# A streaming encoder layer whose five queues are ordered by a pass over the traced instructions, by the longest way to the end

## The chip, the core and the metric

The kernel runs on one core of one Trainium2 chip. A core has five engines with a queue of their own, each worked off in order: TensorE (PE in the profile, with PEld for its weight loads), VectorE (DVE), ScalarE (ACT), GpSimd (POOL) and SyncE (SP), which here issues every DMA. The engines wait for each other through semaphores. The metric is the device time of one execution in microseconds (us), lower being better.

## What is computed

One step of a one-layer hybrid encoder, in float32, for 1024 new tokens of one stream and 32 tokens of a running one, 1056 rows of 1024 numbers:

```python
h = rms_norm(x) @ w_in                      # 15 pieces: q, k, v and gates of three kinds of heads
o_a = gated_linear_scan(q, k, v, log_a)     # GLA, 6 heads:    S_t = diag(a_t) S_{t-1} + k_t v_t^T, o_t = S_t^T q_t
o_b = gated_linear_scan(q, k, v, log_f)     # HGRN2, 5 heads:  the same, wider keys
o_c = mlstm_scan(q, k, v, log_f, ig)        # mLSTM, 5 heads, stabilised by a running maximum
cat = [head_norm(o_a)*silu, head_norm(o_b)*silu, head_norm(o_c)*sigmoid]
x = x + rms_norm(cat @ w_out)
up = causal_conv(rms_norm(x) @ w_up)        # 1024 -> 2 x 2816, width 3
x = x + rms_norm((gelu(gate) * val) @ w_down)
```

The two outputs are returned with all the final states of the recurrences and the convolutions.

## The kernel before

Every big product is made of three matmuls on numbers split into a high and a low half (`mm3`, lines 100 to 102: high by high, high by low, low by high); `split` makes the halves on ACT (L106) and DVE or POOL (L108, L109).

The work runs in stages. `inproj` projects the normed tokens in three groups of 384, 384 and 256+32 tokens: `norm_group` transposes them (tiles xt), `feat` makes 13 feature tiles (PSUM tiles pf, written pf1_6 for group 1, tile 6), and `vg` or `vg_across` eight blocks of values and gates (pv, for group 2 also the transposes pb). Each group's results go to DRAM. `mixer(u, g, ci0)` reads them back for one unit of 128 tokens (u is 0 to 7, and 8 for the 32 tokens of the other stream) and does the scans. Its long part are six levels of scores within a chunk (widths 32, 16, 8, 4, 2, 1; PSUM tiles sc0_32 to sc0_1 for unit 0): for each, DVE and ACT make decayed copies of queries and keys (x, Ld, Qz), PE makes 16 narrow matmuls of 64 rows, and DVE puts them into the score matrix P under a mask (L782). Then come the outputs (og, oh), the mLSTM part (sm, mi, oi, om) and the normed result, cat. The narrow matmuls are issued through `first` and all carry line 692. The tiles that a unit reads (qkb, mqk, v, gt) have one buffer each, the scores one PSUM buffer, and the state goes from one unit to the next, so the units follow each other.

`outproj(p2, W, u)` transposes a unit's cat (ctp), multiplies it with w_out (zp, two halves of 512 columns), norms it, adds x, norms again and transposes for the FFN (fxt). `up_all` makes the up projection by 22 pairs of column tiles and two token halves, each as seven block products (PSUM tiles puy, pux, puw, puz), a convolution on ACT and DVE (y) and the gelu product, stored to h_d. `down_all` reads h_d back and sums over 22 tiles in PSUM (pd).

The order of the work came from two places. The program is written by generators that are pulled in turn: `merge(main, nmain, nside)` advances a list of pending mixers beside the projections, so that group 1 is projected while group 0 is mixed, group 2 while group 1 is mixed, and the output projection runs beside the last units. The scheduler of the tile layer (with `schedule_with_timeline_sim=True`) then lists the instructions of each engine by a simulation of its own, and takes hints from the code: `tc.high_priority(offset=...)` around the narrow matmuls and one logarithm, and `tc.issue_after(ins)`, which keeps a block behind another instruction.

```python
    def first(fn, *args, **kw):
        with tc.high_priority(offset=AHEAD):
            fn(*args, **kw)
```

Of the kernel before, what the change touches and what calls it, by code (L numbers as in the profile page):

```python
# [1 line left out]

# [6 lines left out]
F32 = mybir.dt.float32  # L9
# [3 lines left out]
AF = mybir.ActivationFunctionType  # L13
ALU = mybir.AluOpType
PSUM = bass.MemoryType.PSUM
DRAM = bass.MemoryType.DRAM
# [74 lines left out]
def body(ctx: ExitStack, tc: tile.TileContext, a: dict):  # L91
    nc = tc.nc
    act, dve, pool, pe, sp = nc.scalar, nc.vector, nc.gpsimd, nc.tensor, nc.sync
# [76 lines left out]
    vecs = const("vecs_sb", [128, 12], F32, a["vecs"])  # L170
# [5 lines left out]
    caus, rmask, self_ = cf[:, 0:64], cf[:, 64:448], cf[:, 448:832]  # L176
# [36 lines left out]
    oml = const("oml", [128, 4])  # L213
# [127 lines left out]
    def out_units(g, dst, dst_s, rng, src, smp_off=None, rows=slice(0, 128), drows=None):  # L341

        t0, pl, sl = GROUPS[g]
        u0, nu = t0 // 128, pl // 128
        drows = rows if drows is None else drows
        sp.dma_start(dst[(slice(u0, u0 + nu), drows) + rng].rearrange("u p n -> p u n"),
                     src[rows, :pl].rearrange("p (u n) -> p u n", n=128))
        if sl:
            so = pl if smp_off is None else smp_off
            sp.dma_start(dst_s[(drows,) + rng], src[rows, so:so + sl])  # L350

    def inproj(g, xh, xl, normed, scaled=None):
        t0, pl, sl = GROUPS[g]
        T = pl + sl
# [132 lines left out]
        fr4, e8 = (pf.tile([128, m, T], F32, tag=t, name=f"{t}_{g}", bufs=1) for (t, m) in (("fr", 4), ("e", 8)))  # L487
        e4, fx4, er = e8[:, 0:4], e8[:, 4:7], e8[:, 7]
# [11 lines left out]
                dve.tensor_scalar(fx4[:, f - 1], fx4[:, f - 1], lb[:, f:f + 1], None, op0=ALU.mult)  # L500

        def logs():
            with tc.high_priority(offset=LNA):
                act.activation(e8, e8, AF.Ln, bias=1.0)

        def decays(f, ins):

            with tc.issue_after(ins.ins):
                fr, ls = fr4[:, f], e4[:, f]
                lo = (128, 0, 0, 64)[f]  # L510
                dve.scalar_tensor_tensor(ls, fr, 0.0, ls, op0=ALU.min, op1=ALU.subtract)
                if f:
                    dve.tensor_tensor(fr[lo:], ls[lo:], fr[lo:], op=ALU.subtract)
                    act.activation(fr[lo:], fr[lo:], AF.Exp)
                    dve.tensor_scalar(fr[lo:], fr[lo:], oml[lo:, f:f + 1], None, op0=ALU.mult)
                    dve.tensor_tensor(ls, ls, fx4[:, f - 1], op=ALU.add)
                    out_units(g, qkb_d, qkbs_d, (1, f, slice(None)), fr, None, slice(lo, 128))
                if f in (0, 3):
                    dve.tensor_scalar(ls, ls, vecs[:, 8 + f:9 + f], None, op0=ALU.mult)
                dve.tensor_tensor_scan(ls, rmask[:, :T], ls, 0.0, op0=ALU.mult, op1=ALU.add)  # L520
                out_units(g, qkb_d, qkbs_d, (2, f, slice(None)), ls)

        def store_q(f, q):
            out_units(g, qkb_d, qkbs_d, (0, f, slice(None)), q)
# [84 lines left out]
        for t, f in ((6, 1), (7, 2)):  # L609
            ps = feat(t)  # L610
# [14 lines left out]
        row = rows()  # L625
# [9 lines left out]
        q = t1("q", 2)  # L635
# [19 lines left out]
        for t, j in ((10, 0), (11, 1), (12, 2), (13, 3)):  # L655
            ins = conv(j, feat(t))
# [25 lines left out]
    halves, kwi = [], [None]  # L682
# [4 lines left out]
    AHEAD = 100  # L687
    LNA = 100

    def first(fn, *args, **kw):  # L690
        with tc.high_priority(offset=AHEAD):
            fn(*args, **kw)

    def mixer(u, g, ci0):
        n = 128 if u < 8 else DEC
        t0 = 128 * u
        chunks = [(0, 64), (64, 64)] if u < 8 else [(0, DEC)]
        cl = chunks[0][1]
# [49 lines left out]
        with ExitStack() as behind:  # L748
            if halves:

                for ins in (kwi[0], halves[1]):
                    behind.enter_context(tc.issue_after(ins.ins))
            spread(dve, qz, lambda r, fs, psl: dve.tensor_tensor(qz[r, psl, :n], q4[r, fs, :], eb4[r, fs, :],
                                                                 op=ALU.mult), n)
        kh = mx.tile([128, 512], F32, tag="x", name=f"kh{u}", bufs=NX)
# [3 lines left out]
                          b5, op=ALU.subtract)  # L759
# [31 lines left out]
        for c in levels:  # L791
            x = mx.tile([128, 512], F32, tag="x", name=f"x{u}_{c}", bufs=NX)
# [198 lines left out]

# [110 lines left out]
    def col_operands(pool_, q, s, between=lambda: None):  # L1102

        n = SUBS[s][1]
        res = {}

        def halves(name, src):
            p = pool_[name in ("T2", "T3")]
            h = p.tile([128, 4, n], F32R, name=f"{name}h{s}")
            l = p.tile([128, 4, n], F32R, name=f"{name}l{s}")  # L1110
            res[name] = h, l
            act.copy(h, src)
            return dve.tensor_tensor(l, src, h.bitcast(F32), op=ALU.subtract)
# [375 lines left out]
    p7s.close()  # L1489
    p4s.close()  # L1490

def _layout(i):
# [125 lines left out]
```

## Time and profile before

| what | us |
| --- | --- |
| timed runs, median (lowest to highest of 3) | 1444.28 (1443.7 to 1444.57) |
| profiled execution, span from first to last instruction | 1434.5 |
| PE busy | 1370.8 |
| DVE busy | 1008.9 |
| ACT busy | 713.2 |
| POOL busy | 274.1 |

The span is the time from the first to the last instruction of one profiled execution on the one core; what the timed runs have over it lies before and after. Busy time is the time in which at least one instruction of the engine is under way. The ends of matmuls are modelled, and a matmul's row holds the time until its result is there, so that rows of one engine overlap; the distance of two starts is then the cost of one. A line can be that of a helper: all big products have lines 100 to 102, all narrow ones 692.

### The profile page before, as it was taken

What the parts mean: (1) busy time and instruction counts of PE and PEld (TensorE: products, weight loads), DVE (VectorE), ACT (ScalarE), POOL (GpSimd) and SP (SyncE); (2) the same over time, 40 slices, a digit from 0 to 9 for tenths busy, and PEclk for the clock granted to TensorE, in tenths of its full rate; (3) what the DMA queues carried; (4) which work ended last, traced back from release to release, by engine and by line L of the source; (5) the groups of instructions that cost most, each with busy time, mean ns of one, the idle gap of its engine ahead of it and who ended that gap; (6) DMA issues with size and microseconds to landing.
All of it is one profiled execution on the core that took longest, in us unless ns stands there. A gap on an engine that the chain in (4) does not pass through costs nothing.

```text
span 1434.5 us, 30019 instructions
## 1 busy us (share of the span) xinstructions
PE 1370.8 (96%) x11804; PEld 1254.9 (87%) x11804; DVE 1008.9 (70%) x1826; ACT 713.2 (50%) x1403; POOL 274.1 (19%) x456
## 2 busy tenths in 40 slices
PE   7989999999998998999799999999999999999997
PEld 6989889898887986767699999999999999988785
DVE  5796478757596668676698888788878865654644
ACT  5545556445475545333665555455555545543432
POOL 6531121113021235212111111111111110000101
PEclk9999999999999999999899999999999999999999
DMA  9599778667789754344312221222122266665742
GB/s 344 190 317 351 263 251 300 221 228 241 236 279 329 250 181 148 109 147 111 122 49 98 79 90 61 90 75 82 68 90 75 75 211 227 222 214 170 247 168 103
DMA packets 132437, 255.11 MB, mean 178 GB/s; under 512 B 28647, under 2 KB 79367, under 8 KB 132295
## 3 DMA queue, kind: packets, MB, share of 16 engines
q1 hardware_dynamic: 132295, 253.19, 51.9%
q8 instruction: 92, 1.51, 0.4%
q14 instruction: 50, 0.41, 0.1%
HBM read 192.26 MB, written 60.89 MB: 176 GB/s over the span
## 4 chain that ended last, share of the span: by engine, by line
PE 73%; DVE 12%; ACT 5%; DMA 5%; issue 2%; POOL 1%; SPq 1%; DVEq 0%; ACTq 0%
PE pd L101 5%; PE pd L100 5%; PE pd L102 5%; PE pux L100 4%; PE pux L102 4%; PE pux L101 4%; PE pv L102 4%; PE pv L100 4%; PE pv L101 4%; PE puw L100 3%; PE puw L101 3%; PE puw L102 3%; DMA qkb<-qkb_d 2%; PE zp L100 2%; PE zp L101 2%
## 5 line engine op out<-in xcount | busy, mean ns | idle before, releaser
L1226 DVE SCALAR_TENSOR_TENSOR y<-uu,fconv_sb,y 128x1060 f32<-128x1060 f32 x88 | 116.2, 1321 | 27.4 <-ACT y L1224 26.6
L100 PE MATMUL pd<-wd,hh 128*128 128x512 f32 x264 | 104.5, 396 | 0.3 <-ACT hh L106 0.3
L101 PE MATMUL pd<-wd,hh 128*128 128x512 f32 x264 | 104.7, 397 | 0.0
L102 PE MATMUL pd<-wd,hl 128*128 128x512 f32 x264 | 90.5, 394 | 0.0
L1220 POOL COPY uu<-uu 128x2 f32<-128x2 f32 x44 | 30.5, 693 | 211.5 <-DVE uu L1188 211.4
L1183 ACT COPY c<-pux 128x274 f32<-128x274 f32 (+1 forms) x132 | 49.1, 375 | 41.4 <-PE pux L102 40.3
L1224 ACT ACTIVATE y<-uu,fconv_sb 128x1060 f32<-128x1060 f32 x44 | 56.1, 1275 | 18.6 <-POOL uu L1221 18.1
L100 PE MATMUL zp<-woh,ch 128*128 128x512 f32 (+1 forms) x144 | 58.3, 411 | 4.1 <-DVE cl L1020 3.1
L100 PEld LDWEIGHTS pd<-wd,hh 128*128 128x128 f32 x264 | 49.6, 188 | 13.1 <-ACT hh L106 0.9
L102 PEld LDWEIGHTS pd<-wd,hl 128*128 128x128 f32 x264 | 49.6, 188 | 11.9
L101 PEld LDWEIGHTS pd<-wd,hh 128*128 128x128 f32 x264 | 49.6, 188 | 11.5
L100 PE MATMUL pv<-wt_0h,xh 128*128 128x256 f32 (+2 forms) x195 | 57.1, 293 | 2.3 <-ACT xh L316 2.3
L101 PE MATMUL zp<-wol,ch 128*128 128x512 f32 (+1 forms) x144 | 58.6, 407 | 0.0
L102 PE MATMUL zp<-woh,cl 128*128 128x512 f32 (+1 forms) x144 | 58.0, 406 | 0.2 <-DVE cl L1020 0.2
L102 PE MATMUL pv<-wt_1h,xl 128*128 128x256 f32 (+2 forms) x195 | 56.9, 292 | 0.5 <-DVE xl L317 0.5
L102 PE MATMUL pv<-wt_0h,xl 128*128 128x256 f32 (+2 forms) x195 | 56.5, 290 | 0.6 <-DVE xl L317 0.6
L100 PE MATMUL pv<-wt_1h,xh 128*128 128x256 f32 (+2 forms) x195 | 56.7, 291 | 0.0
L101 PE MATMUL pv<-wt_1l,xh 128*128 128x256 f32 (+2 forms) x195 | 56.5, 290 | 0.0
L101 PE MATMUL pv<-wt_0l,xh 128*128 128x256 f32 (+2 forms) x195 | 56.2, 288 | 0.1
L101 PE MATMUL pd<-hl,wd 128*128 128x288 f32 x176 | 50.3, 297 | 0.6 <-DVE hl L109 0.6
L218 POOL TENSOR_SCALAR hrs<-hss 128x5 f32<-128x5 f32 (+3 forms) x27 | 13.9, 514 | 192.1 <-DVE hss L888 191.4
L102 PE MATMUL pd<-hh,wd 128*128 128x288 f32 x176 | 50.1, 296 | 0.0
(1668 smaller groups left out, 5162.7 us busy)
## 6 DMA issues: line engine op xcount, KB each, us to landing
h_d<-y SPq DMA_DIRECT2D x22, 530.0 KB, 2.9
wt_0r<-in_w_tok SPq DMA_DIRECT2D x21, 512.0 KB, 8.2
wt_1r<-in_w_tok SPq DMA_DIRECT2D x21, 512.0 KB, 5.6
wt_0l<-lt_d SPq DMA_DIRECT2D x14, 512.0 KB, 5.2
wt_1l<-lt_d SPq DMA_DIRECT2D x14, 512.0 KB, 4.6
qkb<-qkb_d SPq DMA_DIRECT2D x8, 768.0 KB, 6.3
hr<-h_d SPq DMA_DIRECT2D x44, 128.0 KB, 3.7
hr<-h_d SPq DMA_DIRECT2D x22, 192.0 KB, 3.3
```

The source lines that it names most:

```text
L100: pe.matmul(ps, lh[0], rh[0], start=first, stop=False, **kw)
L101: pe.matmul(ps, lh[0], rh[1], start=False, stop=False, **kw)
L102: return pe.matmul(ps, lh[1], rh[0], start=False, stop=last, **kw)
L218: pool.tensor_scalar(out, ss, 1.0 / width, EPS, op0=ALU.mult, op1=ALU.add)
L1183: act.copy(t, ps)
L1220: pool.tensor_copy(u[:, GAP_P:GAP_P + 2], u[:, GAP_S - 2:GAP_S])
L1224: act.activation(y, u, AF.Identity, scale=fconv[:, j, 2:3], bias=fconv[:, j, 3:4])
L1226: dve.scalar_tensor_tensor(y, uu[i][:, s:s + NCOL], fconv[:, j, s:s + 1], y, op0=ALU.mult, op1=ALU.add)
```

## The change

Nothing is computed differently. The hints to the scheduler are taken out of the body (what they wrapped stays), and after the body has been traced, `order(nc, tc)` goes over the list of instructions and fixes the whole order of each of the five queues: it adds for each pair of neighbours in the new order a dependency without a semaphore, so that the scheduler has nothing left to choose.

To find the order it builds a graph (`Graph`): each instruction is a node, with edges from reads and writes of the same part of a tile, from the accesses to one PSUM tile, and from the reuse of a tile's buffer by a later one. `_cost` and `_product` give each node a duration by formulas in the file, and `tails` computes for each node the longest way to the end of the program through those edges. `play` then runs through the program in time: each engine, whenever it is free, takes from its ready instructions the one with the longest way to the end. On PE an instruction that needs another tile shape than the last one is put back by `CHANGE` (1000 ns). [...] Only the order that it finds is kept.

```diff
         def logs():
-            with tc.high_priority(offset=LNA):
-                act.activation(e8, e8, AF.Ln, bias=1.0)
+            act.activation(e8, e8, AF.Ln, bias=1.0)
 
         def decays(f, ins):
 
-            with tc.issue_after(ins.ins):
-                fr, ls = fr4[:, f], e4[:, f]
...
+            fr, ls = fr4[:, f], e4[:, f]
...
     def first(fn, *args, **kw):
-        with tc.high_priority(offset=AHEAD):
-            fn(*args, **kw)
+        fn(*args, **kw)
...
                 for ins in (kwi[0], halves[1]):
-                    behind.enter_context(tc.issue_after(ins.ins))
+                    pass
...
-                with tc.issue_after(halves[0].ins):
-                    act.copy(W[1][:, k, :], wo_raw[k])
-                with tc.issue_after(halves[1].ins):
-                    dve.tensor_tensor(W[2][:, k, :], wo_raw[k], W[1][:, k, :].bitcast(F32), op=ALU.subtract)
+                act.copy(W[1][:, k, :], wo_raw[k])
+                dve.tensor_tensor(W[2][:, k, :], wo_raw[k], W[1][:, k, :].bitcast(F32), op=ALU.subtract)
...
-        with tc.issue_after(ins.ins):
-            halves("T3", t3)
+        halves("T3", t3)
...
-            with tc.issue_after(done[0].ins):
-                next(last[i])
+            next(last[i])
...
+CHANGE = 1000.
+ENGINES = ("PE", "DVE", "Activation", "Pool", "SP")
+WINDOW = 3413.3
+PRODUCT = {512: 229.5, 384: 175.5, 288: 133.5, 282: 131.5, 274: 127.5, 256: 117.5}
...
+    def tails(self):
+
+        deg, out = [len(p) for p in self.pred], []
...
+        tail = [0.] * len(out)
+        for n in reversed(out):
+            e, far = self.eng[n], 0.
+            for s in self.succ[n]:
+                lat = 0 if e is None or not self.pred[s][n] or self.eng[s] == e == "PE" else \
+                    2100 + self.cost[n][0] if e == "SP" else 204 if e == "PE" else 34
+                far = max(far, tail[s] + lat)
+            own = self.cost[n][1] if e != "PE" else self.mm[n][0] if self.mm[n][1] else self.mm[n][0] / 3
+            tail[n] = far + own
+        return tail
...
+def play(g, tail, change):
...
+    while True:
+        t, e = min(((free[e] if ready[e] else max(free[e], wait[e][0][0]), k) for k, e in enumerate(ENGINES) if ready[e] or wait[e]),
+                   default=(None, None))
+        if e is None:
+            break
+        e = ENGINES[e]
+        while wait[e] and wait[e][0][0] <= t + 1e-6:
+            heapq.heappush(ready[e], heapq.heappop(wait[e])[1:])
+        if e == "PE" and len(ready[e]) > 1:
+            c = min(heapq.nsmallest(12, ready[e]), key=lambda x: x[0] + (change if mm[x[1]][2] != mode else 0))
+            ready[e].remove(c)
+            heapq.heapify(ready[e])
+        else:
+            c = heapq.heappop(ready[e])
...
+def order(nc, tc):
+
+    g = Graph(nc, tc)
+    seq = play(g, g.tails(), CHANGE)[2]
+    info = mybir.DependencyInfo(mybir.DependencyClass.NoSync, mybir.DependencyReason.DATA)
+    for s in seq.values():
+        for a, b in zip(s, s[1:]):
+            tc.add_manual_dep(g.ins[b], g.ins[a].name, info, reason="order")
...
     with tile.TileContext(nc, **TC) as tc:
         body(tc, args)
+        order(nc, tc)
```

More of the change, by code (lines that the diff above doesn't have):

```diff
@@ L1 @@
+import heapq
 from contextlib import ExitStack
@@ L1490, in body, with _aps, _size @@
     p4s.close()
+CHANGE = 1000.
+ENGINES = ("PE", "DVE", "Activation", "Pool", "SP")
+WINDOW = 3413.3
+PRODUCT = {512: 229.5, 384: 175.5, 288: 133.5, 282: 131.5, 274: 127.5, 256: 117.5}
+PACKET = ((4, 9), (32, 9), (128, 13), (256, 18), (512, 27), (1024, 46), (1536, 65), (2048, 84), (4096, 159), (8192, 330), (1 << 16, 2640))
+TABLES = {"Ln": 5, "Gelu_apprx_tanh": 11, "Exp": 0, "Tanh": 0, "Square": 0}
+def _aps(xs):
+    return [a for a in xs if hasattr(a, "bass_ap")]
+def _size(a):
+    return int(np.prod([x[1] for x in a.ap[1:]]))
@@ new lines, in _in_psum, with _in_dram, _region @@
+def _in_psum(a):
+    return "PSUM" in str(getattr(a.bass_ap.tensor, "space", ""))
+def _in_dram(t):
+    return "DRAM" in str(getattr(t, "space", "DRAM"))
+def _region(t, a):
+    ap, off = [tuple(x) for x in a.ap], a.bass_ap.offset
+    if _in_dram(t):
+        runs = [x for x in ap if x[1] > 1]
+        last = runs.pop()[1] if runs and runs[-1][0] == 1 else 1
+        o = np.array([off], np.int64)
+        for s, c in runs:
+            o = (o[:, None] + np.arange(c)[None] * s).ravel()
+        lo, hi = o // 64, (o + last - 1) // 64
+        w = int((hi - lo).max()) + 1
+        ix = np.minimum(lo[:, None] + np.arange(w)[None], hi[:, None]).ravel()
+        p0, p1 = 0, 128
+    else:
+        p0, o0 = divmod(off, int(np.prod(t.shape[1:])))
+        p1 = p0 + ap[0][1]
+        ix = np.array([o0], np.int64)
+        for s, c in ap[1:]:
+            if c > 1:
+                ix = (ix[:, None] + np.arange(c)[None] * s).ravel()
+    b = np.zeros(int(ix.max()) // 8 + 1, np.uint8)
+    np.bitwise_or.at(b, ix >> 3, (1 << (ix & 7)).astype(np.uint8))
+    return p0, p1, int.from_bytes(b.tobytes(), "little")
@@ new lines, in _cost, with run @@
+def _cost(i, e):
+    ins, op = _aps(i.ins), i.opcode
+    n = max((_size(a) for a in ins + _aps(i.outs)), default=1)
+    ps = any(_in_psum(a) for a in ins + _aps(i.outs))
+    src = [a for a in ins if _size(a) > 1 and not _in_psum(a)]
+    scal = sum(1 for a in ins if _size(a) == 1) if n > 1 else 0
+    if e == "DVE":
+        single = not ps and len(src) < 2
+        lock = 1 if len(src) > 1 or (not ps and op in ("TensorCopy", "TensorScalarPtr")) else 0
+        if op == "TensorScalarPtr" and i.is_tensor_tensor_scan:
+            d, lock = 142 + 2.11 * n, 1
+        elif op == "CopyPredicated":
+            s, c = i.outs[0].ap[-1]
+            inner = c if s == 1 else 1
+            d = 385 if n <= 100 else 950 if n > 400 else 940 if inner <= 2 and n > 300 else 530 if n > 300 or inner <= 2 else 326
+        elif op == "Reciprocal":
+            d = 45 + 29 * n
+        elif op == "Memset":
+            d = 58 + .834 * n
+        elif single and op in ("TensorCopy", "TensorScalarPtr"):
+            d = 156 + .514 * n + 62 * scal
+        elif op == "TensorScalarPtr":
+            d = (165 if ps else 150) + 1.04 * n + 65 * scal
+        else:
+            d = (148 if ps else 155) + 1.04 * n
+        return d, max(d - 82, 20), lock
+    if e == "Activation":
+        d = (155 if ps else 192 if op == "TensorCopy" else 200) + .838 * n + 92 * (0 if op == "TensorCopy" else scal)
+        return d, d + (60 if len(i.outs) > 1 else -98), 0
+    if e == "Pool":
+        if op == "TensorTensor":
+            d = (550 if n == 1 else 320 + 169 * n) if str(i.op).endswith("pow") else \
+                194 if n == 1 else (108 if str(i.op).endswith("subtract") else 179) + 2.2 * n
+        else:
+            d = 99 + .835 * n if op == "Memset" else 190
+        return d, max(d - 65, 20), 1 if src else 2 if ins else 0
+    if e == "SP":
+        def run(a):
+            r = 1
+            for s, c in reversed([tuple(x) for x in a.ap][0 if _in_dram(a.bass_ap.tensor) else 1:]):
+                if c > 1:
+                    if s != r:
+                        break
+                    r *= c
+            return r
+        el, tot = min(run(i.outs[0]), run(i.ins[0])), int(np.prod([x[1] for x in i.outs[0].ap]))
+        w = float(np.interp(el * 4, [x[0] for x in PACKET], [x[1] for x in PACKET]))
+        return max(1, tot // el) * w / 16 * 1.15, 390 + (80 if len(i.outs[0].ap) > 2 else 0), 0
+    return 0, 0, 0
@@ new lines, in _product @@
+def _product(i):
+    n, mode = _size(i.outs[0]), tuple(i.tile_size)
+    f32, tr = str(i.ins[0].dtype).endswith("float32"), bool(i.is_transpose)
+    r, c = i.tile_position
+    cells = [x * 4 + y for x in range(r // 32, (r + mode[0]) // 32) for y in range(c // 32, (c + mode[1]) // 32)]
+    t, off = i.outs[0].bass_ap.tensor, i.outs[0].bass_ap.offset
+    bank = (t.name, off % int(np.prod(t.shape[1:])) // 512)
+    sums = [(bank, x) for x in range(c // 32, (c + mode[1]) // 32)]
+    if mode == (128, 128) or (mode == (128, 32) and not f32) or mode == (32, 128):
+        g = PRODUCT.get(n, n / 2.4 + 12) if not f32 else max(n * 2 / 2.4 + 2.5, 60) if tr else 2 * max(n * 2 / 2.4 + 8, 112)
+        return g, True, (128, 128) if mode == (128, 32) else mode, cells, (r, sums)
+    return (2 if tr else 4) * n / 2.4 + (5 if tr else 10), False, mode, cells, (r, sums)
@@ new lines, with __init__, factor, add @@
+class Clock:
+    def __init__(self):
+        self.busy, self.cold, self.done = {}, {0}, 0
+    def factor(self, t):
+        k = int(t // WINDOW)
+        while self.done < k:
+            self.done += 1
+            if self.busy.get(self.done - 1, 0) < .39 * WINDOW:
+                self.cold.add(self.done)
+        return 2. if k in self.cold else 1.
+    def add(self, t, work):
+        k = int(t // WINDOW)
+        self.busy[k] = self.busy.get(k, 0) + work
+    def run(self, t, work):
+        while work > 0:
+            f, end = self.factor(t), (int(t // WINDOW) + 1) * WINDOW
+            part = min(work, (end - t) / f)
+            self.add(t, part)
+            work -= part
+            t = t + part * f if work <= 0 else end + 1e-6
+        return t
```

210 lines of the change are left out of this document (198 added, 12 removed).

## Prediction

> **What bounds the kernel now.** I read first the page's busy times, then a table of busy time by stage, then what TensorE waits for, and last the pace of the mixers. The profiled execution has a span of 1434.5 us; the median of the timed runs is 1444.28, so 9.8 us lie around the span, and I add them at the end.
>
> The engine row of the page:
>
> ```profile
> PE 1370.8 (96%) x11804; PEld 1254.9 (87%) x11804; DVE 1008.9 (70%) x1826; ACT 713.2 (50%) x1403; POOL 274.1 (19%) x456
> ```
>
> TensorE (PE) is busy 96% of the span, so reordering alone, which removes no matmul, can win at most the 63.7 us in which it is idle, plus what changes of tile shape cost inside the busy time. Where those 63.7 us lie is told by the table of stretches. The columns are the stretch, its length, then busy time and instructions of PE, of weight loads, DVE, ACT and POOL, the granted clock, the DMA share and GB/s. I cut the span by the names of the tiles: A to 154 (input projections of group 0), B to 345 (projections of group 1, mixers of group 0), C to 516 (projections of group 2, mixers of group 1), D to 680 (output projection, last mixers), E to 728 (change-over to the FFN), F to 1166 (up projection), G (down projection), and the end.
>
> ```profile
> 0.00:154.00 154.00, 135.76 (x919) 130.04 (x920) 105.29 (x155) 79.62 (x142) 61.93 (x65) 0.99 0.87 302
> 154.00:345.00 191.00, 187.53 (x2187) 171.15 (x2186) 132.73 (x311) 101.11 (x204) 39.06 (x56) 0.99 0.73 246
> 345.00:516.00 171.00, 162.82 (x2093) 147.08 (x2092) 118.05 (x323) 93.15 (x219) 35.78 (x51) 0.98 0.77 259
> 516.00:680.00 164.00, 154.78 (x1510) 118.45 (x1509) 117.83 (x248) 69.20 (x154) 46.80 (x68) 0.96 0.44 143
> 680.00:728.00 48.00, 35.47 (x208) 31.71 (x207) 36.27 (x42) 32.18 (x66) 8.31 (x16) 0.86 0.28 91
> 728.00:1166.00 438.00, 438.00 (x3575) 438.00 (x3574) 356.59 (x515) 224.37 (x388) 68.44 (x169) 1.00 0.23 82
> 1166.00:1425.60 259.60, 256.39 (x1326) 218.45 (x1324) 136.31 (x228) 112.29 (x228) 10.87 (x26) 1.00 0.61 200
> 1425.60:1434.50 8.90, 0.00 (x0) 0.00 (x0) 5.83 (x10) 1.27 (x4) 2.88 (x6) 0.79 0.46 178
> ```
>
> F and G, half of the span, have nothing to give: PE is idle 0.0 and 3.2 us there. The rest is A 18.2, B 3.5, C 8.2, D 9.2, E 12.5 and the end 8.9. What ends PE's own idle time:
>
> ```profile
> PE xt L314 <- DVE x L303: 7.8, 1, 7.8
> PE pb L444 <- ACT vf L456: 4.0, 1, 4.0
> PE pf L100 <- DVE q L533: 3.4, 1, 3.4
> PE zp L100 <- DVE cl L1020: 3.1, 3, 2.7
> PE puz L101 <- DVE T4l L1113: 3.0, 1, 3.0
> ```
>
> The largest, 7.8 us, is the load and the scaling of the first 128 rows; no order removes it. The others are single waits of 3 to 4 us.
>
> **What the change does, part by part.** No engine gets or loses an arithmetic instruction; the order of all five queues is new. Three places show what matters.
>
> On PE, the last of unit 0's score matmuls (sc0_1; unit 0 is the mixer of the first 128 tokens) stood among group 1's feature projections (pf1_6). Before:
>
> ```order
> L100 MATMUL pf1_6_2067<-xh1_1715,wf1_6h_2063 128x384
> L692 MATMUL sc0_1_2200<-Qz1_151,qkb0_1779 64x2x32 x4
> L692 MATMUL sc0_1_2200<-Qz1_151,qkb0_1779 64x32 x8
> L692 MATMUL sc0_1_2200<-Qz1_151,qkb0_1779 64x2x32
> L692 MATMUL sc0_1_2200<-Qz1_151,qkb0_1779 64x32
> L692 MATMUL sc0_1_2200<-Qz1_151,qkb0_1779 64x2x32
> ```
>
> Now:
>
> ```order
> L315 MATMUL xt70_4414<-ident_121,x7_3912 128x128
> L690 MATMUL mi_157<-v0_1786,kt2_153 32x64 x6
> L690 MATMUL sc0_1_2200<-Qz1_151,qkb0_1779 64x2x32 x4
> L690 MATMUL sc0_1_2200<-Qz1_151,qkb0_1779 64x32 x8
> L690 MATMUL sc0_1_2200<-Qz1_151,qkb0_1779 64x2x32
> L690 MATMUL sc0_1_2200<-Qz1_151,qkb0_1779 64x32
> ```
>
> They moved behind all of group 1's projections, next to the transposes of unit 7's input (xt70). So stage B loses its mixers. In narrow mixer matmuls on PE's queue, B held 627 and now holds 72, C 687 and now 973, D 442 and now 713 (stages cut at the first pv3_0, pv6_0, zp00 and puy0_0). With 207 to a full unit (1756 over 8.5 units, the unit of 32 tokens counted as half), B loses 2.7 units, C wins 1.4 and D 1.3. Nothing else crosses a stage.
>
> What a unit costs on PE, from the stretches for line 692 alone:
>
> ```profile
> 154.00:345.00 191.00, 50.88 (x1233) 40.59 (x1233) 0.99 0.73 246
> 345.00:516.00 171.00, 50.93 (x1277) 40.52 (x1277) 0.98 0.77 259
> 516.00:680.00 164.00, 40.85 (x975) 32.12 (x975) 0.96 0.44 143
> ```
>
> 142.66 us over 8.5 units is 16.8 us a unit. A change of tile shape costs about 0.10 us more than the next matmul of the same shape, by these rows (a wide product follows a wide one after 0.13 us, but after 0.23 us on either side of the narrow group):
>
> ```profile
> 168.74 0.30 PE L101 MATMUL pv<-wt_1l,xh 128*128 128x282 f32 x1
> 168.97 0.58 PE L692 MATMUL sc<-Qz,Ld 64*64 64x64 f32 x24
> 170.03 0.40 PE L102 MATMUL pv<-wt_1h,xl 128*128 128x282 f32 x1 [0.48 <-DVE xl L317]
> 170.26 0.29 PE L100 MATMUL pv<-wt_1h,xh 128*128 128x282 f32 x1
> 170.39 0.29 PE L101 MATMUL pv<-wt_1l,xh 128*128 128x282 f32 x1
> ```
>
> Shape changes on the queue go from 349 to 320: by stage, A 8 and 8, B 129 and 14, C 140 and 176, D 72 and 122. So PE's need is: B 187.5 - 2.7 x 16.8 - 115 x 0.1 = 131; C 162.8 + 1.4 x 16.8 + 36 x 0.1 = 190; D with E 190.3 + 1.3 x 16.8 + 50 x 0.1 = 217. Their sum falls by 3 us only. The work is moved, not removed; the question is whether C and D can be kept as full as they were.
>
> DVE does not forbid it. In the fastest unit of the trace (next fence) DVE was busy 27.8 us with everything, so C gets at most 118 + 1.4 x 27.8 = 157 us in some 190 (83%), D with E 154 + 36 = 190 in 217 (88%). That is fuller than the 69% and 73% of before.
>
> The **pace of the mixers** is the tight term. One unit's block of gates and queries (qkb) has one buffer, so a unit starts when the one before has made its last scores; the starts are the exponentials of line 743, and the last row is the stretch of the fastest full unit, columns as in the table of stages:
>
> ```profile
> 198.66 0.64 ACT L743 ACTIVATE eb<-qkb 128x512 f32<-128x512 f32 x1 [7.07 <-DMA qkb<-qkb_d]
> 268.05 0.63 ACT L743 ACTIVATE eb<-qkb 128x512 f32<-128x512 f32 x1 [0.56 <-DMA qkb<-qkb_d]
> 323.62 0.64 ACT L743 ACTIVATE eb<-qkb 128x512 f32<-128x512 f32 x1 [1.98 <-DMA qkb<-qkb_d]
> 384.56 0.64 ACT L743 ACTIVATE eb<-qkb 128x512 f32<-128x512 f32 x1 [7.23 <-DMA qkb<-qkb_d]
> 448.75 0.63 ACT L743 ACTIVATE eb<-qkb 128x512 f32<-128x512 f32 x1 [7.78 <-DMA qkb<-qkb_d]
> 490.41 0.31 ACT L743 ACTIVATE eb<-qkb 128x128 f32<-128x128 f32 x1 [2.99 <-DMA qkb<-qkbs_d]
> 589.05 0.64 ACT L743 ACTIVATE eb<-qkb 128x512 f32<-128x512 f32 x1 [5.77 <-DMA qkb<-qkb_d]
> 448.80:490.40 41.60, 37.17 (x553) 33.04 (x553) 27.82 (x75) 22.63 (x52) 8.08 (x9) 0.96 0.91 340
> ```
>
> Seven periods from 198.66 to 589.05 are 55.8 us each; the fastest full one, 448.75 to 490.41, took 41.7. In C there are now 4.7 units: to hide behind PE's 190 us they must go at 40.4 us each, which no unit of this trace reached. I take 42.5, next to the fastest, because the slow ones were spread out by the hand-written merge and had PE busy beside them, not because their own chain was that long. Then C takes 4.7 x 42.5 = 200 us, 10 more than PE's need. In D the 3.4 units take 145 us of 217 and are covered; the idle time of D and E (21.7) I leave at 16, since single waits there (2.7 and 3.0 above) are of the kind that an order avoids.
>
> At the last mixer PE has little to fill with. Before, around unit 7's scores of width 4 and 2:
>
> ```order
> L692 MATMUL sc7_4_8177<-Qz1_151,Ld1_149 64x32
> L1016 MATMUL ctp41_8134<-ident_121,ct4_7848 128x128 x4
> L692 MATMUL mi_157<-cf_sb_110,x7_0_8234 128x11 x4
> L1080 MATMUL fxt30_8195<-ident_121,z3_7782 128x128 x4
> L1080 MATMUL fxt31_8201<-ident_121,z3_7782 128x128 x4
> ```
>
> Now:
>
> ```order
> L690 MATMUL sc7_4_8177<-Qz1_151,Ld1_149 64x32
> L1012 MATMUL ctp50_8439<-ident_121,ct5_8121 128x128 x4
> L1012 MATMUL ctp51_8448<-ident_121,ct5_8121 128x128 x4
> L690 MATMUL sc7_2_8216<-Qz0_150,Ld0_148 64x2x32 x4
> L690 MATMUL mi_157<-cf_sb_110,x7_0_8234 128x11 x4
> ```
>
> Both have only transposes there, no products: this wait stays, and is in the 16.
>
> In A the projections of two feature tiles are now interleaved, so a wait of one is covered by the other: of the 18.2 I keep 7.8 and about 5. But SP's first rows change too, with a weight load between the first rows (x0) and their gain (gx). Before:
>
> ```order
> L151 DMA x0_90<-in_xp 128x1024
> L162 DMA gx_92<-in_grows 128x1024
> L151 DMA x1_94<-in_xp 128x1024
> ```
>
> Now:
>
> ```order
> L152 DMA x0_90<-in_xp 128x1024
> L169 DMA wt0_0_0r_96<-in_w_tok0 128x846
> L163 DMA gx_92<-in_grows 128x1024
> ```
>
> gx is what the first scaling waits for, so PE's first matmul may come up to the queue's step later; half a microsecond to nothing, inside A's term. The waits taken out with the old hints (the issue_after blocks) cost nothing by themselves; the list replaces them.
>
> Added semaphore waits: PE's instructions that only wait go from 105 to 125 in the built queues, DVE's from 499 to 463. One takes 17 ns where the trace shows it,
>
> ```profile
> L743 ACTq EVENT_SEMAPHORE  x2: 17/17/17, 323.6 to 490.3; - x2
> ```
>
> so 20 more are 0.3 us at most; I leave them at zero.
>
> **The sum**, against the span: A 154 to 149 (-5); B 191 to 132 (-59); C 171 to 200 (+29); D with E 212 to 233 (+21); F 0; G -1; the end -2, because the last six sums in PSUM no longer finish together. -17, and -3 that I expect where the interleaving also shortens A's and E's half-clock stretches (clock 0.86 in E's row; 48 us at 0.86 are worth up to 6.7). Together -20: span 1414.5, and with the 9.8 around it **1424 us**.
>
> **The rivals.**
> (1) The mixers keep up, C costs PE's 190 and D with E 225: -10 and -8 more, 1406. For it: the list knows the tile shapes, the clock and the buffers; against it: the 40.4 us a unit that no row shows. The low end of the range is this case with all of the idle time gone but the first 7.8 us and half of the end (63.7 - 7.8 - 4.5 = 51) and 3 us of shape changes: 1390. In D's row weight loads take 118.45 of 164 us, matmuls 154.78. [...]
>
> (2) Slower: **the mixers decide C**. Each microsecond of period above 42.5 costs 4.7 us; above 46.8 the whole gain is gone. At 50 us a unit C is 235 and the time 1424 + 35 = 1459. For it: the average pace was 55.8, and each unit waits 6 to 7 us for its qkb load in full view; a matmul that waits at the head of PE's queue holds all the products behind it. Against it: B and C had PE busy 98 and 95%, so the mixers were not pressed before. The granted clock was 0.86 in E and 0.96 in D, against 1.00 in F. [...]
> (3) F loses its lockstep: PE is busy 438.00 of 438.00 with DVE at 356.6, and DVE's queue is re-sorted there too. 0.5 us in each of 44 blocks is 22 us: 1446, no gain.
> (4) The order is not taken up: excluded, the queues do differ.
>
> **Chances.** Forecast, 1412 to 1438: 0.47. Rival 1: 0.18. Rival 2: 0.20. Rival 3: 0.15, half of it on each side of no change. A difference under 0.2% (2.9 us) cannot be told here. Faster: 0.47 + 0.18 + 0.04 = 0.69; the same 0.08; slower 0.23. The range, 1390 to 1452, leaves out the worse half of rival 2.
>
> **What would show it.** Right: stage B, up to the first pv6_0, shrinks to about 132 us with PE over 97% busy and DVE near half; starts of eb from unit 1 on about 42 us apart; F still 438 us. Wrong: periods over 47 us with PE waiting on Qz or P in C (rival 2); PE idle in F behind uu or c1 (rival 3); C at 190 (rival 1).

## The result, and the profile after

The changed kernel takes 1435.7 us (median of 4 runs, 1434.53 to 1436.78) beside 1444.4 us for the kernel before on the same chip: a ratio of 0.9935 with an interval of 0.992 to 0.9949. Run again later on another occasion, the same two kernels stood at 0.9955 (0.9941 to 0.9969). So the order is worth 6.5 to 9 us, where 20 were forecast. The direction was right, the size was less than half of it.

The engine row of the page after is that of before almost to the digit: TensorE (PE) is busy 1370.8 us in both. Whatever was won lies outside it or was given back inside it.

```profile
PE 1370.8 (96%) x11804; PEld 1251.0 (87%) x11804; DVE 1010.2 (71%) x1826; ACT 716.8 (50%) x1403; POOL 268.4 (19%) x456
```

The table of stretches after, with the columns of the table before (stretch, length, busy time and instructions of PE, weight loads, DVE, ACT and POOL, granted clock, DMA share, GB/s). The cuts are those of the second table below, so B now ends near 293, C near 494 and the change-over near 710; the prediction's cuts of the trace before lie up to 12 us beside the same events:

```profile
0.00:154.00 154.00, 136.58 (x916) 131.24 (x917) 102.36 (x150) 78.22 (x134) 57.95 (x63) 0.98 0.90 301
154.00:293.00 139.00, 137.84 (x1060) 133.06 (x1058) 58.62 (x116) 73.93 (x132) 14.27 (x32) 1.00 0.86 286
293.00:494.00 201.00, 191.91 (x2823) 167.68 (x2821) 169.46 (x439) 120.78 (x277) 52.87 (x68) 0.99 0.76 250
494.00:680.00 186.00, 173.74 (x1925) 131.59 (x1926) 142.94 (x335) 74.16 (x188) 56.96 (x79) 0.94 0.46 140
680.00:710.00 30.00, 20.41 (x105) 17.88 (x103) 23.68 (x28) 20.60 (x40) 7.62 (x13) 0.77 0.35 112
710.00:1163.00 453.00, 451.60 (x3642) 448.93 (x3641) 363.99 (x524) 227.17 (x401) 63.45 (x171) 1.00 0.23 79
1163.00:1424.40 261.40, 258.61 (x1344) 220.61 (x1342) 145.19 (x233) 120.85 (x232) 14.17 (x29) 1.00 0.63 202
1424.40:1432.70 8.30, 0.16 (x1) 0.00 (x0) 3.93 (x6) 1.13 (x4) 1.13 (x4) 0.82 0.33 127
```

B is the forecast stage: 139 us in place of 191, PE busy 99% of it, DVE 42%. C and D are longer by what left B. But F (710 to 1163) has 453 us where it had 446 between the same events, and though PE is called busy in nearly all of it, its work cannot have grown. What PE waited for, longest first:

```profile
PE xt L315 <- DVE x L304: 9.7, 1, 9.7
PE pux L101 <- ACT c L1178: 5.4, 2, 4.6
PE puw L103 <- DVE S_0h L110: 3.7, 1, 3.7
PE mi L589 <- ACT r_dc L576: 3.5, 1, 3.5
PE ctp L1012 <- DMA ct<-cat_d: 3.1, 1, 3.1
```

They are other waits than before, and sum to about as much: PE's idle time is 61.9 us where it was 63.7. The first matmul comes at 9.7 in place of 7.8. The mixers' starts:

```profile
306.18 0.64 ACT L741 ACTIVATE eb<-qkb 128x512 f32<-128x512 f32 x1 [1.38 <-DMA qkb<-qkb_d]
342.54 0.63 ACT L741 ACTIVATE eb<-qkb 128x512 f32<-128x512 f32 x1 [0.46 <-DMA qkb<-qkb_d]
386.11 0.63 ACT L741 ACTIVATE eb<-qkb 128x512 f32<-128x512 f32 x1 [2.37 <-DMA qkb<-qkb_d]
429.95 0.63 ACT L741 ACTIVATE eb<-qkb 128x512 f32<-128x512 f32 x1
...
602.54 0.63 ACT L741 ACTIVATE eb<-qkb 128x512 f32<-128x512 f32 x1
```

Seven periods from 306.18 to 602.54 are 42.3 us each, against the 42.5 that were assumed.

For the rest of the text the stages are measured between matmuls, so that two executions can be compared to a tenth: A to unit 3's first transpose (xt), B to unit 6's, C to the first zp, D with E to the last fxt, F to the first pd, then G with the end. The kernel before and the kernel after were each profiled twice (the second times are the runs e1_before and e9_after below):

| stage | forecast | before, two executions | after, two executions | difference of means |
| --- | --- | --- | --- | --- |
| A | -5 | 157.0, 156.5 | 156.4, 155.9 | -0.6 |
| B | -59 | 190.0, 194.2 | 136.6, 137.4 | -55.1 |
| C | +29 | 180.4, 184.4 | 201.4, 201.8 | +19.2 |
| D with E | +21 | 188.6, 185.1 | 215.5, 215.0 | +28.4 |
| F | 0 | 445.9, 445.8 | 452.9, 453.1 | +7.1 |
| G and end | -3 | 272.6, 272.8 | 269.9, 268.4 | -3.6 |
| clock | -3 | in the stages | in the stages | |
| span | -20 | 1434.5, 1438.8 | 1432.7, 1431.8 | -4.4 |

B, C and D with E together were forecast at -9 and came to -7.5. What is missing is A, F, and the clock. How that sum falls to C and to D with E depends on the cut: the prediction ended C at 516, the table ends it at the first zp, which came at 527.4. In length C came out as forecast, 201.4 us for 200.

### The profile page after: what moved, and what is told of

It reads as the page before. It is cut to its first block, busy times and chain, and to the rows that moved or that the text cites. A ratio compares the mean times of both kernels' runs of the same rounds, so it can differ in the third digit from the quotient of the medians.

```text
span 1432.7 us, 29995 instructions
## 1 busy us (share of the span) xinstructions
PE 1370.8 (96%) x11804; PEld 1251.0 (87%) x11804; DVE 1010.2 (71%) x1826; ACT 716.8 (50%) x1403; POOL 268.4 (19%) x456
## 4 chain that ended last, share of the span: by engine, by line
PE 47%; DMA 2%; DVE 1%; ACT 1%; issue 0%; POOL 0%; SPq 0%; DVEq 0%; POOLq 0%; ACTq 0%
PE pd L101 5%; PE pd L103 5%; PE pd L102 5%; PE pux L101 5%; PE pux L103 4%; PE pux L102 4%; PE puw L101 3%; PE puw L103 3%; PE puw L102 3%; PE puy L101 2%; PE puy L102 1%; PE puy L103 1%; PE puz L101 1%; PE puz L102 1%; PE puz L103 1%; DMA wd_5r<-in_w_dn 1%
## 5 line engine op out<-in xcount | busy, mean ns | idle before, releaser
L101 PE MATMUL pd<-wd,hh 128*128 128x512 f32 x264 | 78.0, 397 | 1.5 <-ACT hh L107 1.5
L102 PE MATMUL pd<-wd,hh 128*128 128x512 f32 x264 | 77.4, 396 | 0.0
L103 PE MATMUL pd<-wd,hl 128*128 128x512 f32 x264 | 77.0, 396 | 0.0
L110 DVE TENSOR_TENSOR hl<-hr,hh 128x384 fp32r<-128x384 f32 (+1 forms) x66 | 34.4, 522 | 44.9 <-PE pd L103 28.3
L1178 ACT COPY c<-pux 128x274 f32<-128x274 f32 (+1 forms) x132 | 45.7, 379 | 26.3 <-PE pux L103 22.3
L107 ACT CAST hh<-hr 128x384 fp32r<-128x384 f32 (+1 forms) x66 | 32.0, 486 | 49.2 <-PE pd L102 30.9
L101 PE MATMUL zp<-woh,ch 128*128 128x512 f32 (+1 forms) x144 | 52.6, 419 | 0.8 <-ACT vth L113 0.8
L1216 POOL COPY uu<-fcache_sb 128x2 f32<-128x2 f32 x44 | 16.6, 377 | 194.4 <-DVE uu L1183 194.4
L102 PE MATMUL zp<-wol,ch 128*128 128x512 f32 (+1 forms) x144 | 52.9, 419 | 0.0
L1279 POOL TENSOR_TENSOR gss<-gss 128x1 f32<-128x1 f32 (+1 forms) x9 | 6.6, 739 | 245.9 <-ACT gjk L1275 245.9
L424 POOL TENSOR_TENSOR vg<-vth,gh 128x256 f32<-128x256 f32 (+1 forms) x36 | 30.6, 850 | 115.8 <-DVE vth L421 56.8
```

The lines of the kernel that those rows point to most:

```text
L101: pe.matmul(ps, lh[0], rh[0], start=first, stop=False, **kw)
L102: pe.matmul(ps, lh[0], rh[1], start=False, stop=False, **kw)
L103: return pe.matmul(ps, lh[1], rh[0], start=False, stop=last, **kw)
L107: act.copy(hi, src)
L110: (eng or pool).tensor_tensor(lo, src, hi.bitcast(F32), op=ALU.subtract)
L424: pool.tensor_tensor(o[:n], th[:n], gh[:n, c0:c0 + 256], op=ALU.mult)
```

## The experiments

**The kernel before, once more.** No edit. My sum added 9.8 us that "lie around the span".

> The kernel before once more, unchanged, to see its profile beside timed runs. Theory 1 (the profiled execution shown of before was a short one): its timed runs stay near 1444, a new profiled execution has a span near 1442.6, that is 1.8 us under its own time as the changed kernel's runs show (1434.53 with a span of 1432.7), and the 8 us more lie in few places, above all in stretches where TensorE's clock is granted at half. Rival (what lies around the span is 9.8 us for this kernel): span again near 1434.5 at a time of 1444.

Measured: 1442.7 us (10 runs, ratio 1.0002, 0.999 to 1.0015), the profiled execution 1440.62 with a span of 1438.8:

```profile
span 1438.8 us, 30019 instructions
PE 1374.2 (96%) x11804; PEld 1258.5 (87%) x11804; DVE 1009.8 (70%) x1826; ACT 713.5 (50%) x1403; POOL 271.1 (19%) x456
```

In all 76 further executions of the kernels before and after whose span is on record, it is 1.7 to 1.9 us under the time. What I took for time around the span was an execution out of the ordinary: its 1434.5 is shorter than each of the 64 other executions of this kernel here, whose spans go from 1436.0 to 1447.1 with a mean of 1440.5; why it was so short stays open. The twelve of the kernel after go from 1431.0 to 1436.3, mean 1433.7. So the gain is 6.8 us by the means of many, 1.8 by the two profiles that one sees first. The theory holds in that, not in the place: the half-clock stretches, in which the trace has half of the clock granted (0.50 from 95.2 to 102.0 in that of after), cost 22 us in the second execution and 21 in the first (each matmul's spacing there less the median spacing of its like); it is longer by 4.2 in B and 4.0 in C, and shorter by 3.5 in D with E.

**Slack in the list's own run, the front alone, the back alone.** The trace after shows in F what the page cannot: around 821 us, one of the first products after a copy of its sum (the columns are start, duration, then engine, line and what is done; c is ACT's copy of the sum pux):

```profile
820.95 0.66 ACT L1178 COPY c<-pux 128x274 f32<-128x274 f32 x2 [0.19 <-PE pux L103]
...
821.44 0.19 PEld L103 LDWEIGHTS puz<-T4h,A_5h 128*128 128x128 f32 x1
...
821.55 0.29 PE L103 MATMUL puz<-T4h,A_5h 128*128 128x274 f32 x1
821.67 0.19 PEld L101 LDWEIGHTS pux<-T2h,S_5h 128*128 128x128 f32 x1
821.68 0.37 PE L101 MATMUL pux<-T2h,S_5h 128*128 128x256 f32 x1
821.78 0.19 PEld L102 LDWEIGHTS puw<-B22l,S_5h 128*128 128x128 f32 x1
...
821.89 0.29 PE L102 MATMUL puw<-B22l,S_5h 128*128 128x274 f32 x1
```

Here a weight load usually starts 0.11 us ahead of its matmul, under the one before (821.44 for 821.55). The load for pux<-T2h starts at 821.67, 0.06 after ACT's copy is over at 821.61, and 0.01 ahead of its matmul; that matmul then takes 0.37 in place of 0.28, and the next starts 0.21 after it. No wait is on the page, since PE is counted as busy, but 0.09 us are lost. In the middle of F such spacings (0.15 to 0.3 us) are counted 85 times in the trace after, twice in that of before; what they have over 0.125 us sums to 6.3 us. Nearly all are like this one: in 80 places the load starts 0.05 us after the end of ACT's copy c (59) or of DVE's sum uu (21), while from 726 to 1160 of the trace before no load comes less than 0.11 us ahead of its matmul. In the rows above, a load that waits for nothing starts under the matmul before, 0.11 us ahead of its own (821.78 for 821.89), and the one that had to wait is 0.01 ahead. Three kernels take the cause apart (the list is the order that `play` makes):

```diff
 e2_slack, in play():
-                r = end[n] + (94 if eng[s] == "PE" else 34)
+                r = end[n] + (294 if eng[s] == "PE" else 34)
 e3_front, in order(), and the hint on T3 put back from the second pair of the up projection on:
     for s in seq.values():
+        s = [n for n in s if g.ins[n].name in FRONT]
 e4_back, all hints put back:
     for s in seq.values():
+        s = [n for n in s if g.ins[n].name not in FRONT]
```

> The changed kernel with one constant altered: the list's own run through the program counts 294 ns in place of 94 from the end of an instruction of another engine to the TensorE instruction that waits for it, so that such a matmul is listed later, behind 200 ns more of other matmuls. Theory (the list puts the first matmul after a copy of its sum exactly where that copy ends; in the trace after, the weight load of pux<-T2h starts at 821.67 with the copy c over at 821.61, and the next matmul starts 0.21 us after it where 0.125 is usual, about four times in each of 22 pairs of tiles): these gaps go, the up projection takes 446 to 447 us (first to last) in place of 452.9, time about 1429. Rival (the longer pace of the up projection is the mixing of 256- and 274-wide products or of weights, not the waits): 452 again, time 1434 to 1437.

> The list's order only for what is traced up to the second pair of the up projection; behind it the scheduler's own order with its hint on T3 stands, matmul for matmul as in the kernel before. Theory (the front gains about 15 us against timed runs of before, the list loses 7 in the up projection): time 1428 to 1430, up projection 446, no matmul gap of 0.16 to 0.22 us in it. Rival (the front gains nothing but what the profile-to-profile difference of 1.8 us shows, and the up projection is not the list's fault): 1435 to 1437.

> The opposite: hints and the scheduler's order for the front, the list's order only behind the second pair of the up projection, matmul for matmul as in the changed kernel. Theory: the front as before (first sum of the output projection near 527 us), the up projection 453 in place of 446, the down projection and the end 2 to 3 us shorter, time 1447 to 1449. Rival (the loss in the up projection comes from what the front leaves behind, not from the order in it): 1441 to 1444.

Measured: slack 1432.6 us (ratio 0.9929, 0.9906 to 0.9951), where 1429 was expected; front alone 1436.3 (0.9952, 0.9937 to 0.9968), where 1428 to 1430 was expected; back alone 1448.7 (1.0046, 1.0031 to 1.0061), as expected. The same place in the kernel with slack:

```profile
822.73 0.66 ACT L1178 COPY c<-pux 128x274 f32<-128x274 f32 x2 [0.19 <-PE pux L103]
...
823.59 0.19 PEld L101 LDWEIGHTS pux<-T2h,S_5h 128*128 128x128 f32 x1
823.70 0.28 PE L101 MATMUL pux<-T2h,S_5h 128*128 128x256 f32 x1
...
823.82 0.29 PE L101 MATMUL puz<-T4h,A_5h 128*128 128x274 f32 x1
```

Two more matmuls stand between the copy and the product that needs it, the load goes ahead by 0.11, and the next matmul follows after 0.12. How long the up projection takes is read from two rows of each kernel, the end of the first range being the last zp, the start of the second the first pd (first the kernel before, then after, slack, front alone, back alone):

```profile
L102 PE MATMUL zp<-woh,cl x144: 388/391/628, 528.4 to 692.8; 128*128 128x512 f32 x128, 128*32 128x512 f32 x16
L100 PE MATMUL pd<-hh,wd x176: 292/296/398, 1161.9 to 1236.9; 128*128 128x288 f32 x176
```

```profile
L103 PE MATMUL zp<-woh,cl x144: 387/393/628, 499.2 to 686.4; 128*128 128x512 f32 x128, 128*32 128x512 f32 x16
L101 PE MATMUL pd<-hh,wd x176: 293/296/398, 1162.8 to 1234.2; 128*128 128x288 f32 x176
```

```profile
L103 PE MATMUL zp<-woh,cl x144: 387/393/628, 503.7 to 689.8; 128*128 128x512 f32 x128, 128*32 128x512 f32 x16
L101 PE MATMUL pd<-hh,wd x176: 292/296/400, 1159.5 to 1231.8; 128*128 128x288 f32 x176
```

```profile
L103 PE MATMUL zp<-woh,cl x144: 387/392/774, 504.1 to 692.2; 128*128 128x512 f32 x128, 128*32 128x512 f32 x16
L101 PE MATMUL pd<-hh,wd x176: 291/296/442, 1162.3 to 1237.8; 128*128 128x288 f32 x176
```

```profile
L103 PE MATMUL zp<-woh,cl x144: 387/389/628, 533.3 to 697.1; 128*128 128x512 f32 x128, 128*32 128x512 f32 x16
L101 PE MATMUL pd<-hh,wd x176: 292/296/402, 1176.1 to 1247.7; 128*128 128x288 f32 x176
```

469.1, 476.4, 469.7, 470.1 and 479.0 us. With the list's order behind it, an old front loses 10 us in F; with the old order there, a new front loses 1. F's loss is the list's order in F, and 200 ns of slack give most of it back: F alone takes 447.5 us, 5.4 less than after, and of the long spacings 23 are left, nearly all behind uu. The whole time falls by 3 only, since C to E take 2.6 us more and the granted clock is lower (0.981 over the profiled execution, 0.983 in that of after). The front alone misses by the size of the front's gain: 1431.5 was to be expected of the front alone (1435.7, less 7 in F, plus 3 in G), and it stayed at 1436.3.

**The kernel after, once more**, to see whether the half-clock stretches make that difference.

> The changed kernel once more, beside the others on one chip. The list for the front alone gave 1436.3 where the changed kernel's 1435.7 less 7 (up projection) plus 3 (down projection and end) makes 1431.5. Theory (the difference is the half-clock windows, which fall otherwise from execution to execution: their cost in C and D is 10.8 us in the trace after, 18.6 in that of the front-only kernel, 12 to 21 in other runs of nearly the same order): the new profile of the same program has another set of windows in C and D than the first one, and the time is 1434 to 1439. Rival (the program always has the same windows): the same windows within 2 us, 1435 to 1436.

Measured: 1435.5 us (8 runs, 0.9955, 0.9941 to 0.9969). The rival holds for C and D: the cost of the half-clock stretches there is 11.6 us, and was 10.8 in the first profile, and each of the four begins 1 us later than in that profile, as the work does. Two profiles do not show that it is always so: in E one stretch of 13.7 us has become two of 3.4 and 6.8. In the front-only kernel it is 18.6, and its mean granted clock over six executions is 0.9788 against 0.9815 in twelve of the kernel after, which would be 3.9 us of 1434, were PE the bound throughout. TensorE takes its work in the same order in both up to F. Why one of them is granted less clock stays open.

**The first rows of SP.** The gain gx put directly behind x0 again, in the kernel with slack.

```diff
+    first = next(n for n in seq["SP"] if any("gx" in x.bass_ap.tensor.name for x in _aps(g.ins[n].outs)))
+    seq["SP"].remove(first)
+    seq["SP"].insert(1, first)
```

> The kernel with 294 ns of slack (1432.57, ratio 0.9929) with one more edit: on SP's queue the gain gx stands directly behind the first rows x0 again, ahead of the first weight load. Theory (PE is the bound from its first matmul on, so a start 1.9 us later in the trace after, 9.7 in place of 7.8, is paid in full): first matmul at 7.8 to 7.9, time 1430.7, ratio about 0.9916. Rival (the weights are needed as early as the rows, and what is won at the first matmul is waited out at the first projection): first matmul 7.8, ratio 0.993 as without the edit.

Measured: ratio 0.992 (0.9897 to 0.9943), beside 0.9929 without the edit: no difference that can be told. What PE waits for in A:

```profile
PE xt L315 <- DVE x L304: 8.2, 1, 8.2
PE mi L589 <- ACT r_dc L576: 3.5, 1, 3.5
PE pv L101 <- ACT xh L317: 2.7, 1, 2.7
```

The first matmul comes 1.3 us sooner (8.2 for 9.5; 7.8 was expected), the wait for the split rows (xh) grows from 1.3, which it is with slack alone and in the trace after, to 2.7, and A ends at 156.4 where it ended at 155.9. The rival holds in A: the start is not on the path that sets A's end, as far as one profile of each shows.

**The price of a shape change.**

```diff
-CHANGE = 1000.
+CHANGE = 0.
```

> The changed kernel with CHANGE = 0: the list takes the ready matmul with the longest way to the end whatever its tile shape. Shape changes on PE's queue go from 318 to 872 (B 14 to 49, C 175 to 552, D 122 to 264); nothing is left out. By the prediction's price of 0.10 us a change: +55 us, 1491. By what the traces of before and after hold (all changes together cost 52 to 55 us over the spacing of like neighbours for 318 to 347 changes, 0.16 us each): +88 us, 1524. Rival (most changes fall where PE waits anyway): under 1460.

Measured: 1569.3 us (one execution), 133.6 more than the kernel after, 0.24 us for each of the 554 changes more. More than both prices. The stretch C, PE alone, then the middle of it with all columns, and a piece in order of time:

```profile
310.60:613.60 303.00, 297.41 (x2767) 0.88 0.51 163
```

```profile
353.00:528.00 175.00, 174.53 (x1430) 130.34 (x1429) 93.10 (x231) 63.95 (x137) 18.93 (x29) 0.83 0.53 167
```

```profile
385.82 0.44 PE L690 MATMUL mi<-v,kt 128*32 128x64 f32 x6
386.19 0.61 PE L101 MATMUL pf<-xh,wf_3h 128*128 128x288 f32 x1
386.73 0.48 PE L690 MATMUL mi<-v,kt 128*64 128x64 f32 x2
387.13 0.61 PE L103 MATMUL pf<-xh,wf_2l 128*128 128x288 f32 x1
387.67 0.70 PE L690 MATMUL mi<-v,kt 128*64 128x64 f32 x6
```

By the spacings, the changes themselves cost about 67 us more than in the trace after (0.12 each), short stalls of weight loads 19, and the half clock 54: a granted clock of 0.88 in C, with PE busy 297 of 303 us. Idle gaps fell by about 6 us. Without the rule that keeps shapes together the list is 127 us slower than the kernel before.

**The mixers first, and the mixers slower.** Units 0 to 2 taken ahead by every engine; then DVE's copy into P issued twice, with and without the list's knowledge.

```diff
 e7_early, in order():
+    tail = [t + 150000. * (i is not None and i.name in EARLY) for t, i in zip(g.tails(), g.ins)]
 e8_drag, in put():
+            for _ in range(2):
                 dve.copy_predicated(dst, mk.broadcast_to([n, 11, *mk.shape[2:]]), src)
 e10_fixdrag: the same second copy, and in Graph.node()
+        self.cost.append((1, 1, 0) if i is not None and i.name in TWICE else ...
```

> The changed kernel with 150 us added to the way to the end of the mixer instructions of units 0, 1 and 2, so that every engine takes them first as soon as they are ready; narrow mixer matmuls stand 212/830/713 in B/C/D in place of 74/985/713, shape changes 334 in place of 318. Theory (where the mixers lie changes nothing in itself, PE's need is the same in all stages; what counts is that no stage waits): C is relieved by 0.7 units, 1433 to 1440. Rival 1 (late mixers are the gain, because a mixer taken first breaks the products apart): 1450 or more. Rival 2 (mixers decide C and D): C shorter by 0.7 x 42 = 30 us less what B grows by, 1420 to 1430.

> The changed kernel with DVE's masked copy of the scores into P (L780, 53 of them, 0.55 us in the middle and 0.96 for the widest) issued twice over, the second time to no effect: about 4.5 us more on each unit's own chain, 38 us of DVE in all; the list plans with it. Rival 2 of the prediction (the mixers decide C and D, each microsecond of a unit's period is paid 4.7 times in C and 3.4 in D): periods 46 to 47, time +30 to +36, 1466 to 1472. Theory (the mixers are covered by PE's products as long as DVE has room, 84% in C and 77% in D in the trace after): periods grow by 2 to 4, time +5 to +12, 1441 to 1448.

> The second, idle copy of the scores into P again, but the list does not know of it (it counts 1 ns), so that the order stays that of the changed kernel: narrow matmuls 74/1005/693 in B/C/D, where the planned version had moved 227 into B. Theory (a list that knows of 38 us more on DVE moves the mixers forward and hides them; a fixed order cannot): periods of a unit 45 to 47, time +10 to +25 over the changed kernel, 1446 to 1461. Rival 2 of the prediction with its full price (4.5 us x 8.1 units): +36, 1472. Rival (the mixers have room in any order): within 4 us of the changed kernel.

Measured: mixers first 1465.1 us (1.015, 1.0125 to 1.0174); second copy planned 1436.7 (0.9963, 0.9945 to 0.998); second copy not planned 1445.1 (1.0024, 1.0009 to 1.0039). Mixers taken first are dear, 29 us: 18 of them lie in half-clock stretches, some 13 in shape changes and idle gaps together. The size is that of rival 1 of this run; its reason, products broken apart, was not singled out. A planned copy of 4.5 us a unit costs 1 us, less than the 5 that were expected at least, since the list begins unit 1 at 282.9 in place of 306.2. The first and the last start of the seven periods with it:

```profile
282.87 0.64 ACT L741 ACTIVATE eb<-qkb 128x512 f32<-128x512 f32 x1 [1.65 <-DMA qkb<-qkb_d]
...
593.48 0.63 ACT L741 ACTIVATE eb<-qkb 128x512 f32<-128x512 f32 x1 [4.45 <-DMA qkb<-qkb_d]
```

They are 44.4 us each, 2 longer than without the copy. Not planned, in an order near that of the changed kernel, the copy costs 9.5 us. The starts then, first and last of the same seven periods:

```profile
306.48 0.64 ACT L741 ACTIVATE eb<-qkb 128x512 f32<-128x512 f32 x1
...
607.94 0.64 ACT L741 ACTIVATE eb<-qkb 128x512 f32<-128x512 f32 x1 [3.59 <-DMA qkb<-qkb_d]
```

43.1 us a period for 42.3: of 4.5 us more on DVE a unit takes up 3.8 without growing. 9.5 us is 2.1 for each microsecond added to a unit's work, not the 8.1 that was expected by rival 2, which took the whole addition for a longer period. The period's own 0.7 us a unit, at 8.1, would be 6. My lowest figure here (10) was just missed, and the periods of 45 to 47 were not seen.

**The hints taken out, without the list.**

```diff
         body(tc, args)
-        order(nc, tc)
```

> The body of the changed kernel, hints taken out, without the list: the scheduler's own order. Narrow matmuls 614/718/436 in B/C/D and 325 shape changes, almost as before (633/693/442 and 347). Theory (the hints were worth little in the front and hold the lockstep of the up projection by the one on T3): up projection 2 to 10 us longer than 469 (last zp to first pd), time 1444 to 1455. Rival (the hints carried nothing): 1441 to 1444.

Measured: 1455.0 us (1.0093, 1.0072 to 1.0113). The time is at the end of what was expected, the place is another: the up projection takes 466.6 us (712.7 to 1179.3), not longer but 2.5 shorter; the loss is in the front, where A takes 165.8 (157 before) and C 192.1 (180 and 184).

```profile
0.00:165.80 165.80, 140.21 (x944) 135.20 (x945) 107.41 (x156) 81.60 (x144) 60.72 (x66) 0.95 0.82 284
712.70:1179.30 466.60, 456.95 (x3691) 455.41 (x3690) 376.92 (x537) 243.47 (x428) 77.88 (x181) 0.99 0.24 82
```

So the hints that the change takes out were worth 12.8 us. The list wins 19.4 over the bare scheduler and shows 6.6.

**Both findings in one kernel.** Slack as above, and the list counts the copy into P double though it is issued once.

```diff
-            d = 385 if n <= 100 else 950 ... else 326
+            d = 2 * (385 if n <= 100 else 950 ... else 326)
```

> The changed kernel with two prices of the list altered: 294 ns of slack into TensorE, and DVE's masked copy into P counted double (nothing is issued twice). The order is near that of the kernel with the real second copy: narrow matmuls 239/888/645 in B/C/D, 296 shape changes in place of 318. Theory (planning DVE with room leaves the mixers early enough and makes fewer shape changes, 22 x 0.16 = 3.5 us): 1427 to 1431. Rival (half-clock windows and shape changes come out the same whatever the list believes): 1432 as with the slack alone.

Measured: 1428.9 us (6 runs), ratio 0.9911 (0.9887 to 0.9935): the best of all, twice the gain of the change on the same occasion. Its interval overlaps that of the slack alone, so what the second edit adds is not shown.

## Why the prediction was right in direction and wrong in size

- **B, C, D with E** (-59, +29, +21): right as a sum, -9 for -7.5. By the table C came out 10 us better and D with E 7 worse, but the forecast cut C 11 us ahead of the table's event; only the sum can be judged. The price of a unit's narrow matmuls (16.8) holds: L690 takes 138.8 us of the trace after in B to D, 16.3 a unit.
- **F, 0 us: the step that failed first.** I read "PE busy 438.00 of 438.00" as a stage that had nothing to give, priced it at nothing, and kept its loss for rival 3. It lost 7.1 us. It is near that rival, at a third of its size: operands come late, not by 0.5 us in each of 44 blocks but by 0.07 in 85 places, 6.3 us, and without the idle time of PE that the prediction gave as the rival's sign. Slack in the list's own run takes most of it away.
- **A, -5.** It became -0.6. The list did remove waits: those behind the first matmul sum to 7.5 us and were 10.4 before. But the first matmul came 1.9 later, not "half a microsecond to nothing" (most of which the run with gx moved took back, with A no shorter), and a new wait of 3.5 us appeared, of the kind that I said an order avoids: a tiny matmul (mi, L589) at the head of PE's queue behind ACT's r_dc, with products behind it.
- **The clock, -3.** Not seen. The half-clock stretches cost 21 and 22 us in the two profiles of before, 23 and 17 after. I counted a gain on a resource that no row tied to the interleaving; it varies from 17 to 33 us in twelve of the fourteen traces, with 41 for the mixers first and 76 for CHANGE = 0. What in an order sets it stays open.
- **G and the end, -3**: -3.6, right.
- **The idle time of D and E, 21.7 to 16**: it stayed at 21.9. The large waits of E only changed their names (pux behind c 4.6 and puw behind S_0h 3.7, where it was puz behind T4l 3.0 and pux behind c 2.7). That the last unit's chain sets them, and not the order, is my reading and was not tested.
- **The 9.8 us around the span** are 1.8; a single execution was taken for the typical one.
- **The pace of the mixers.** The numbers were right: 42.3 us a period, C 201 us long with PE busy 191.9, for 42.5, 200 and 190. That a unit's own chain is the tight term is not borne out: of 4.5 us more on DVE 3.8 find room in the period, and a list that knows of them pays 1 us in all by starting the mixers sooner. What ends PE's 9 us of idle time in C was not taken apart. Of the seven waits for qkb that the prediction calls "6 to 7 us" its own rows have four of 5.8 to 7.8, the others 0.6 to 3.0.
- **0.10 us a shape change** holds for the change itself (0.12), and leaves out the 54 us of half clock and the 19 us of short load stalls that came with 554 more of them in the kernel with CHANGE = 0.
- **The weight loads in D** again take less than the matmuls, 131.59 us for 173.74 of 186 (118.45 for 154.78 of 164 before). No order here used the difference, and what it is worth was not shown.

The sum of the missed terms: 7.1 (F), 4.4 (A) and 3 (clock) are 14.5 of the 15.6 us between -20 and the -4.4 of the mean profiles. F's cause is shown by the three kernels above; those of A and the clock are read from the traces and not tested.

## What to carry to other kernels

A list schedule places an instruction at the moment at which its own model says that the operand is there; give each edge into a saturated engine the slack by which a late operand hurts (here 0.2 us into TensorE brought back 5.4 of F's 7.1, and 3 of the whole time), or the stage that was full pays for the others. Look for such losses in the spacing of the matmuls, since busy time does not show them (PE is counted busy for 451.60 of F's 453 us here, and 6.3 of them are lost in such spacings). And before a forecast is made against one profiled execution, ask where it lies among the timed ones.

## What the runs showed of the hardware that was not expected

- In C of the kernel with CHANGE = 0 the granted clock is 0.88, although PE is never long idle: it is busy 98%, and the longest time between the starts of two matmuls is 2.6 us. From 353 to 528 that time is 0.5 us, PE is busy 174.53 of 175 us, and the clock is 0.83. Narrow and wide matmuls alternate there; whether that sets the clock was not tested.
- Half-clock stretches are 3.4, 6.8 or 13.7 us long in the traces of before and after, multiples of 3.4, but for the last one of each, in which the program ends (5.8 us before, 5.0 after).
- The weight load that had to wait (821.67 in the trace after) started 0.01 us ahead of its matmul in place of 0.11, and 0.09 us of PE were lost with no idle time in the profile; 85 such spacings in F have 6.3 us.
